# A streaming encoder step on one core: the square of a tile joins the sum one tile later, the remainder of a weight quarter is emitted with the next cast, and the planner prices a transfer by its pieces

## The chip, the cores and the metric

The kernel runs on one NeuronCore of a Trainium2 chip. The time is the device time of one launch in microseconds (us). Before the change the median of three runs is 1416.33 us (1415.28 to 1420.74). Five engines work beside each other, each through its own queue in order: TensorE (PE in the profile, with its weight loads as PEld), VectorE (DVE), ScalarE (ACT), GpSimd (POOL) and SyncE (SP), which here issues most transfers. A transfer that SP issues also waits in SP's queue for what it needs, and holds up what stands behind it.

## The reference, cut to what matters

One step of a two-layer encoder for two request groups with shared weights: 256 new frames of one stream and 32 of another, 288 columns together, at a width of 2048.

- Layer 0: adaLN (a modulation `silu(c) @ w_mod`, then RMSNorm times scale plus shift), one wide input projection, eight heads of attention with a forget gate and eight of differential attention, SiLU gates, one output projection, and `x = x + gate * out`.
- Layer 1: adaLN again, a projection to `u` and `z`, a diagonal complex state space over the positions, GELU, a GLU product, an output projection, and the residual add.
- A last RMSNorm. Every RMSNorm needs the sum of the squares of `x` over its 2048 channels:

```python
def _rmsnorm(x, g):
    x32 = x.astype(jnp.float32)
    y = x32 * lax.rsqrt(jnp.mean(x32 * x32, axis=-1, keepdims=True) + EPS)
    return (y * g.astype(jnp.float32)).astype(x.dtype)
```

All is float32, and the tolerance needs nearly that.

## The kernel before, in words

Activations lie transposed: channels on the 128 partitions, the 288 columns along the free dimension, so a width of 2048 is 16 tiles of 128x288. Full precision comes from splitting each operand into a rounded part and its remainder: a weight quarter `st[:, i, :]` (128x512) becomes `hi`, which ACT casts, and `lo = w - hi`, which DVE subtracts; an activation chunk becomes `ah` and `al` in the same way. One product of a 128x128 weight block with an activation tile is then three matmuls (`ah,hi`, `al,hi`, `ah,lo`). Here such a triple is called a step. The five projections hold 2304 steps in all, and a place in the program is given below as the number of steps that stand before it in PE's order: the input projection of layer 0 is steps 0 to 1024, its output projection 1024 to 1280, the projection to `u` and `z` 1280 to 1792, the GLU product 1792 to 2048, the last projection 2048 to 2304.

A job is 16 steps with one weight tile of 1 MB (four quarters). `pump` issues the loads of the next jobs on SP as soon as one of the four slots is free; a slot is free when the `lo` of its fourth quarter is done (`st_done`). `split_step` casts the quarters ahead of PE; eight `hi`/`lo` pairs may be alive. Between the steps `side.step` lets side tasks (Python generators) emit a piece of their work: the modulation's tail, the softmax heads, the builder of the state-space matrices (`v`, `w_ps`, `k_ps`), and in layer 1 the state space itself.

What sets the order is a planner, `Plan`. Every instruction is entered with an assumed cost as it is emitted, and each engine and the pool of DMA engines has an assumed clock. A side task is let on when the assumed time of what it waits for is past on PE's assumed clock, and when the assumed clock of DVE or ACT isn't more than 4 us ahead of PE's (`BACKLOG`). The engines then run these orders as they stand, with semaphores; the assumed times have no other effect.

The state space in layer 1 goes by groups of four tiles. `u` is written to DRAM (`ud<-MX`) and read back in two forms: regrouped in eight transfers with runs of 36 numbers (`MX<-ud`), for the products `xin_ps`; and as lagged copies (`UL<-ud`, later `W1r<-ud`, four a tile), for the products `t_ps`. DVE then runs the recurrence over `X` (`X<-X,t` and `t<-X,rot`, some hundred small instructions a group), ACT gathers `Xm`, PE makes `y_ps`, ACT copies it into `Yg`, eight transfers write that to DRAM (`yd<-Yg`), two read it back (`yx<-yd`), and GELU follows on DVE and ACT. The GLU product needs all of it, split into `ah` and `al` in four chunks; its first group of columns takes chunk 3 from step 1840 on. `xin_ps`, `t_ps` and `y_ps` stand in PE's queue between the steps of the projection, so a late transfer stops the projection too.

The output projection of layer 0 (`op_evac`) and the last projection (`fin_evac`) add each finished tile to `MX` with two DVE instructions, square the tile on ACT (`yx<-MX`), and add the square to `ssq1` on DVE. Four PSUM banks (`pm`) hold the tiles in progress: PE can't begin a fifth before DVE has emptied the first. `h1_task` then scales a chunk of `MX` into `ah` and `al` for the projection to `u` and `z`.

In the profile every instruction has line 114, since one helper (`Engine.__getattr__`) records them all; groups are told apart by their tiles.

Of the kernel before, what the change touches and what calls it, by code (L numbers as in the profile page):

```python
# [93 lines left out]
class Engine:  # L94
# [5 lines left out]
    def __getattr__(self, fn):  # L100
# [14 lines left out]
        return call  # L115

    def cost(self, fn, out, ins, outs, k):
        p = self.plan
# [3 lines left out]
        if fn == "dma_start":  # L122
            t = max([p.when(p.written, a) for a in ins] + [p.at[self.name], p.base.get(out.tensor.name, 0.0)])
            p.at[self.name] = t + (0.45 if self.name != "pool" else 1.0)
            size = n * out.shape[0] * 4 / 360e3
            if self.name == "act":
                end = t + 2.6 + 2 * size
            else:
                p.at["dma"] = max(p.at["dma"], t + 0.6) + size
                end = p.at["dma"] + 2.0  # L130
            p.note(p.written, out, end)
            for a in ins:
                p.note(p.read, a, end)
            p.last = max(p.last, end)
            return
# [118 lines left out]
def build(tc, I, O):  # L254
# [8 lines left out]
    with ExitStack() as ctx:  # L263
# [23 lines left out]
        def TT(o, a, b, op, eng=dve):  # L287
            eng.tensor_tensor(o, a, b, op=op)
# [107 lines left out]
        def st_done(k):  # L396
            del st_of[k]
            if taken and taken[0] is None:
                taken[0] = slot_of[k]
            else:  # L400
                st_free.append(slot_of[k])
# [4 lines left out]
        def split_step(t, force=False):  # L406
# [12 lines left out]
            act.copy(hi, st[:, i, :])  # L419
            TT(lo, st[:, i, :], hi.bitcast(F32), ALU.subtract)  # L420
            qs.append((hi, lo))
            split["live"] += 1
            if i == 3:
                st_done(k)
                pump()
            return True

        def order_of(j):
# [21 lines left out]
        def run_jobs(upto, n_side):  # L450
            while pos["run"] < upto:
# [5 lines left out]
                if j["kind"] == "main":  # L457
# [6 lines left out]
                    for i, (n, q, k, begin, end) in enumerate(order_of(j)):  # L464
                        while len(qs) <= q:
                            if not qs:
                                side.upto(plan.when(plan.written, st_of[t]))
                            split_step(t, True)
                        if first and begin:
                            g["ps"][n] = pm.tile([128, 512], F32, tag="m", name="m")  # L470
# [7 lines left out]
                        if last and end:  # L478
                            plan.last = 0.0
                            g["evac"](n, ps[:, 0:N], c)  # L480
                        if i % 2:
                            split_step(t)
                            side.step(n_side)
# [106 lines left out]
        def slot(k):  # L590
            return k if k < 12 else k + 4
# [753 lines left out]
        def op_evac(gi):  # L1345
            def ev(n, ps, c):
# [9 lines left out]
                if c == 3:  # L1356
                    sq = scratch(k % 2)[:, 0:T]
                    act.activation(sq, MX[:, slot(k), :], AF.Square)
                    if k == 0:
                        dve.tensor_copy(ssq1, sq)  # L1360
                    elif k < KT - 1:
                        TT(ssq1, ssq1, sq, ALU.add)
                    else:
                        ssl.append(sq)
                    if n == 3:
                        ready.add(("x1", gi))
            return ev

        ssl = []
        op0 = len(jobs)  # L1370
# [408 lines left out]
        def fin_evac(gi):  # L1779
            def ev(n, ps, c):  # L1780
# [3 lines left out]
                for b, (j0, j1) in enumerate(((0, JP), (JP, NJ))):  # L1784
                    dve.scalar_tensor_tensor(xk[:, :, j0:j1], ps.rearrange("p (s j) -> p s j", s=LC)[:, :, j0:j1],
                                             gate[:, 1, k, b:b + 1], xk[:, :, j0:j1], op0=ALU.mult, op1=ALU.add)
                sq = scratch(k % 2)[:, 0:T]
                act.activation(sq, MX[:, k, :], AF.Square)
                if k == 0:
                    dve.tensor_copy(ssq1, sq)  # L1790
                elif k < KT - 1:
                    TT(ssq1, ssq1, sq, ALU.add)
                else:
                    ssl.append(sq)
            return ev
# [192 lines left out]
```

## Time and profile before

| | before |
|---|---|
| median of 3 runs | 1416.33 us |
| profiled execution, its own time | 1416.64 us |
| its span, first to last instruction | 1414.8 us |
| PE busy | 1270.3 us (90%) |
| DVE busy | 928.9 us (66%) |
| ACT busy | 594.3 us (42%) |
| mean granted TensorE clock | 0.948 |
| DMA, mean over the span | 244 GB/s |

Engine rows give busy time, its share of the span and the number of instructions. A row of waits reads: the engine and tile that stood idle, what released it, total idle in us, number of waits, the longest. A row of the timeline gives start and length in us, the engine, the operation with output and inputs, the count of merged instructions, and in brackets the idle time before it with its releaser. SPq is SP's sequencer, which issues transfers. A step takes three rows of `m` on PE.

### The profile page before, as it was taken

To read this page: it belongs to the slowest core of one execution; us is meant where nothing else is said; L and a number is where in the kernel's file an instruction comes from. 1 tells how busy PE (TensorE), PEld (TensorE's weight loads), DVE (VectorE), ACT (ScalarE), POOL (GpSimd) and SP (SyncE) were. 2 spreads that over 40 slices of the span, in tenths; PEclk is the share of its full clock that TensorE was granted. 3 is DMA by queue.
4 is the path that set the end of the run, shared out by engine and by line. 5 is a ranking of instruction groups with operands and counts; after the bars stand their busy time and mean duration, and the time that the engine had idled before them with its cause. 6 is when DMAs were issued, how large, how long until landed. Compare 5 with 4: busy or idle time off the path is not lost.

```text
span 1414.8 us, 28189 instructions
## 1 busy us (share of the span) xinstructions
PE 1270.3 (90%) x11098; PEld 1112.1 (79%) x11098; DVE 928.9 (66%) x2212; ACT 594.3 (42%) x1394; POOL 32.6 (2%) x21
## 2 busy tenths in 40 slices
PE   4999899999998999998996978849979877999996
PEld 2788798887887888886896958838869847989995
DVE  4479988697786777887667618527735835455554
ACT  4434233333454454554535624413444534344341
POOL 0005000000000000000000000000000000000000
PEclk9999999999999999999998999978988978999998
DMA  9988696698889898987755877883587645877641
GB/s 316 339 304 309 211 329 249 227 336 293 313 289 312 287 317 298 337 296 271 272 178 137 287 200 174 226 205 104 181 188 201 197 150 155 293 258 266 230 148 68
DMA packets 251011, 344.91 MB, mean 244 GB/s; under 512 B 51424, under 2 KB 141552, under 8 KB 250880
## 3 DMA queue, kind: packets, MB, share of 16 engines
q1 hardware_dynamic: 238208, 313.47, 68.5%
q10 hardware_dynamic: 12672, 29.65, 5.9%
q8 instruction: 88, 1.44, 0.4%
q14 instruction: 43, 0.35, 0.1%
HBM read 307.13 MB, written 35.95 MB: 242 GB/s over the span
## 4 chain that ended last, share of the span: by engine, by line
issue 46%; PE 24%; DVE 13%; DMA 10%; ACT 4%; SPq 1%; ACTq 0%; POOL 0%; POOLq 0%; DVEq 0%
PE m L114 19%; DMA w<-in_w_in_att 5%; DVE lo L114 4%; PE mod_ps L114 3%; DVE v L114 2%; ACT hi L114 2%; DVE MX L114 2%; DMA w<-in_w_mod 2%; DVE tmpv L114 1%; DMA w<-in_w_out_att 1%; SPq L114 1%; DVE qkv L114 1%; DVE dtmp L114 1%; DMA v_d<-v 1%; DMA c_gT<-in_gT 0%
## 5 line engine op out<-in xcount | busy, mean ns | idle before, releaser
L114 PE MATMUL m<-ah,hi 128*128 128x288 f32 (+1 forms) x2304 | 717.2, 311 | 28.3 <-ACT ah L114 14.6
L114 PE MATMUL m<-ah,lo 128*128 128x288 f32 (+1 forms) x2304 | 691.8, 300 | 6.7 <-DVE lo L114 6.6
L114 PE MATMUL m<-al,hi 128*128 128x288 f32 (+1 forms) x2304 | 692.6, 301 | 0.4 <-DVE al L114 0.4
L114 DVE TENSOR_TENSOR lo<-w,hi 128x512 fp32r<-128x512 f32 x560 | 374.2, 686 | 246.3 <-ACT hi L114 236.0
L114 PEld LDWEIGHTS m<-ah,hi 128*128 128x128 f32 x2304 | 444.3, 193 | 94.9 <-issue 41.8
L114 ACT CAST hi<-w 128x512 fp32r<-128x512 f32 x560 | 326.5, 618 | 362.5 <-PE m L114 204.0
L114 PEld LDWEIGHTS m<-ah,lo 128*128 128x128 f32 x2304 | 444.9, 193 | 9.3 <-DVE lo L114 9.3
L114 PEld LDWEIGHTS m<-al,hi 128*128 128x128 f32 x2304 | 445.2, 193 | 1.6 <-DVE al L114 1.4
L114 PE MATMUL mod_ps<-w,cs 128*32 128x512 f32 x736 | 96.2, 617 | 1.9 <-DMA w<-in_w_mod 1.9
L114 DVE SCALAR_TENSOR_TENSOR qkv<-m,qkv 128x288 f32<-128x288 f32 x168 | 73.0, 452 | 26.4 <-PE m L114 26.1
L114 DVE TENSOR_TENSOR X<-X,t 128x32 f32<-128x32 f32 (+1 forms) x256 | 58.3, 228 | 8.2
L114 PE MATMUL t_ps<-UL,kb 128*32 128x288 f32 (+1 forms) x220 | 31.9, 431 | 26.1 <-DMA UL<-ud 26.1
L114 ACT ACTIVATE yx<-MX 128x288 f32<-128x288 f32 (+1 forms) x40 | 19.7, 492 | 70.0 <-DVE MX L114 70.0
L114 DVE TENSOR_TENSOR v<-pt,raw 128x512 f32<-128x512 f32 (+1 forms) x64 | 46.0, 718 | 2.5 <-DMA v_d<-v 2.2
L114 DVE SCALAR_TENSOR_TENSOR MX<-MX,c_dT,t_ps 128x288 f32<-128x288 f32 x16 | 8.2, 514 | 59.0 <-PE t_ps L114 59.0
L114 DVE TENSOR_TENSOR tmpv<-pt,raw 128x512 f32<-128x512 f32 (+1 forms) x64 | 45.9, 717 | 0.0
L114 PE MATMUL y_ps<-Xm,v 128*128 128x74 f32 x256 | 37.4, 309 | 9.1 <-ACT Xm L114 9.1
L114 PEld LDWEIGHTS y_ps<-Xm,v 128*128 128x128 f32 x256 | 35.9, 223 | 10.8 <-ACT Xm L114 10.3
L114 PEld LDWEIGHTS t_ps<-UL,kb 128*32 128x32 f32 x220 | 9.5, 124 | 43.6 <-DMA UL<-ud 35.2
L114 DVE SCALAR_TENSOR_TENSOR MX<-m,gate,MX 128x256 f32<-128x256 f32 x96 | 30.7, 362 | 18.7 <-PE m L114 18.6
L114 PEld LDWEIGHTS mod_ps<-w,cs 128*32 128x32 f32 x736 | 16.9, 110 | 29.4 <-issue 25.6
L114 DVE TENSOR_TENSOR v<-v,tmpv 128x512 f32<-128x512 f32 (+1 forms) x48 | 34.3, 714 | 1.7
(228 smaller groups left out, 921.1 us busy)
## 6 DMA issues: line engine op xcount, KB each, us to landing
w<-in_w_mod SPq DMA_DIRECT2D x128, 512.0 KB
w<-in_w_in_att SPq DMA_DIRECT2D x40, 1024.0 KB
w<-in_w_in_ssm SPq DMA_DIRECT2D x32, 1024.0 KB
w<-in_w_mod SPq DMA_DIRECT2D x28, 1024.0 KB
w<-in_w_in_att SPq DMA_DIRECT2D x48, 512.0 KB
w<-in_w_out_att SPq DMA_DIRECT2D x16, 1024.0 KB
w<-in_w_glu SPq DMA_DIRECT2D x15, 1024.0 KB
w<-in_w_out_ssm SPq DMA_DIRECT2D x13, 1024.0 KB
```

The lines of the kernel that those rows point to most:

```text
L114: return f(*a, **k)
```

## The change

It has three parts. (1) The `lo` subtraction of a quarter isn't emitted behind its `hi` cast any more, but is kept in `rests` and emitted at the next cast, or as soon as the planner's time for the cast is past on DVE's or PE's assumed clock (`rest_due`), or at the latest ahead of the first matmul that reads it. The release of the slot and the next load move with the fourth quarter's `lo`. (2) `squares` emits the add of a tile's square ahead of the next tile's square instead of behind its own; the first square goes straight into `ssq1`, so the copy is gone; the last one is handed on as before. (3) The planner's price of a transfer no longer is its bytes at 360 GB/s, but the number of its contiguous pieces, each at 12 plus 0.142 per number, over 16 engines; and it lets a transfer begin 1.2 instead of 0.6 us after its issue, or end 3.2 instead of 2.6 us after it on ACT's queue. For a 1 MB weight tile the price goes from 2.91 to 2.71 us, for one of the eight transfers with runs of 36 numbers from 0.205 to 0.547 us. The instructions that are executed stay the same, but for the two copies; their order on PE, DVE, ACT and SP is new over the whole program.

```diff
+    @staticmethod
+    def pieces(out, src):
+
+        total, run = 1, []
+        for d in out.shape:
+            total *= d
+        for a in (out, src):
+            r = 1
+            for st, n in reversed(list(a.ap)[1:]):
+                if st != r and n > 1:
+                    break
+                r *= n
+            run.append(r)
+        r = min(run)
+        return total / r * (12 + 0.142 * r) / 16e3
...
-            size = n * out.shape[0] * 4 / 360e3
+            size = self.pieces(out, ins[0])
             if self.name == "act":
-                end = t + 2.6 + 2 * size
+                end = t + 3.2 + 2 * size
             else:
-                p.at["dma"] = max(p.at["dma"], t + 0.6) + size
+                p.at["dma"] = max(p.at["dma"], t + 1.2) + size
                 end = p.at["dma"] + 2.0
...
             act.copy(hi, st[:, i, :])
-            TT(lo, st[:, i, :], hi.bitcast(F32), ALU.subtract)
             qs.append((hi, lo))
             split["live"] += 1
-            if i == 3:
-                st_done(k)
-                pump()
+            rest_step(0)
+            rests.append((k, i, st, hi, lo))
             return True
+        rests = []
+        def rest_step(left):
+            while len(rests) > left:
+                k, i, st, hi, lo = rests.pop(0)
+                TT(lo, st[:, i, :], hi.bitcast(F32), ALU.subtract)
+                if i == 3:
+                    st_done(k)
+                    pump()
+        def rest_due():
+            if rests and plan.when(plan.written, rests[0][3]) <= max(plan.at["dve"], plan.at["pe"]):
+                rest_step(len(rests) - 1)
...
+                        if rests and rests[0][:2] <= (t, q):
+                            rest_step(0)
...
                         if i % 2:
+                            rest_due()
                             split_step(t)
                             side.step(n_side)
...
-                    sq = scratch(k % 2)[:, 0:T]
-                    act.activation(sq, MX[:, slot(k), :], AF.Square)
-                    if k == 0:
-                        dve.tensor_copy(ssq1, sq)
-                    elif k < KT - 1:
-                        TT(ssq1, ssq1, sq, ALU.add)
-                    else:
-                        ssl.append(sq)
+                    squares(k, MX[:, slot(k), :])
...
+        def squares(k, x):
+            for sq in sqs:
+                TT(ssq1, ssq1, sq, ALU.add)
+            sqs.clear()
+            sq = scratch(k % 2)[:, 0:T] if k else ssq1
+            act.activation(sq, x, AF.Square)
+            if k == KT - 1:
+                ssl.append(sq)
+            elif k:
+                sqs.append(sq)
```

What this does to the orders is shown at three places.

DVE at the end of layer 0's output projection, where the finished tiles are added to `MX` and their squares (`yx`) to `ssq`. Before:

```order
L114 SCALAR_TENSOR_TENSOR MX<-m,gate,MX 128x8x32
L114 SCALAR_TENSOR_TENSOR MX<-m,gate,MX 128x8x4
L114 TENSOR_TENSOR ssq_123<-ssq_123,yx 128x288
L114 SCALAR_TENSOR_TENSOR MX<-m,gate,MX 128x8x32
L114 SCALAR_TENSOR_TENSOR MX<-m,gate,MX 128x8x4
L114 TENSOR_TENSOR ssq_123<-ssq_123,yx 128x288
L114 TENSOR_TENSOR lo<-w,hi 128x512
```

Now:

```order
L114 TENSOR_TENSOR lo<-w,hi 128x512
L114 SCALAR_TENSOR_TENSOR MX<-m,gate,MX 128x8x32
L114 SCALAR_TENSOR_TENSOR MX<-m,gate,MX 128x8x4
L114 TENSOR_TENSOR lo<-w,hi 128x512
L114 SCALAR_TENSOR_TENSOR MX<-m,gate,MX 128x8x32
L114 SCALAR_TENSOR_TENSOR MX<-m,gate,MX 128x8x4
L114 TENSOR_TENSOR ssq_123<-ssq_123,yx 128x288
L114 SCALAR_TENSOR_TENSOR MX<-m,gate,MX 128x8x32
```

The rows look alike, but the first add now stands behind the third tile of the sum, and reads the square of the second: the square that an add reads was begun a tile earlier. Two chunk rows (`al<-MX,scl,ah`) of `h1_task` have also moved: of the first chunk's four tiles one stood ahead of step 1280 before, and all four do now.

SP around the second write of `u` to DRAM. Before:

```order
L114 DMA ud<-MX 128x4x288
L114 DMA UL<-ud 128x1x288 x3
L114 DMA w<-in_w_in_ssm 128x4x512 x2
L114 DMA MX<-ud 16x32x36 x8
L114 DMA UL<-ud 128x1x288
```

Now:

```order
L114 DMA ud<-MX 128x4x288
L114 DMA UL<-ud 128x1x288
L114 DMA w<-in_w_in_ssm 128x4x512
L114 DMA kb<-kb_d 128x256
L114 DMA MX<-ud 16x32x36 x8
```

One weight load less stands between the write and the eight transfers that read it back. At the third write it is none instead of one.

PE around step 1792, the end of the projection to `u` and `z`. Before, behind the last `m` of 290 columns:

```order
L114 MATMUL y_ps<-Xm,v_12894 128x74 x8
L114 MATMUL t_ps<-UL,kb 32x288 x4
L114 MATMUL t_ps<-UL,kb 32x144 x4
L114 MATMUL t_ps<-UL,kb 32x288
L114 MATMUL t_ps<-W1r,kb 32x288 x3
L114 MATMUL t_ps<-UL,kb 32x144
L114 MATMUL t_ps<-W1r,kb 32x144 x3
L114 MATMUL y_ps<-Xm,v_13544 128x74 x8
L114 MATMUL t_ps<-UL,kb 32x288 x4
L114 MATMUL t_ps<-UL,kb 32x144 x4
```

Now the last `t_ps` stands 16 steps ahead of that place, between steps of the projection:

```order
L114 MATMUL y_ps<-Xm,v_12670 128x74 x8
L114 MATMUL t_ps<-UL,kb 32x288
L114 MATMUL t_ps<-W1r,kb 32x288 x3
L114 MATMUL t_ps<-UL,kb 32x144
L114 MATMUL t_ps<-W1r,kb 32x144 x3
L114 MATMUL m<-ah,hi 128x290
L114 MATMUL m<-al,hi 128x290
L114 MATMUL m<-ah,lo 128x290
```

Four `t_ps` tiles and two `y_ps` tiles stood at step 1792 with no step of a projection among them. Now the `t_ps` of tiles 10 to 15 stand at steps 1702, 1718, 1722, 1740, 1770 and 1776 (before: 1774, 1780 and four at 1792), and the `y_ps` of tiles 12 to 15 at 1776, 1780, 1788 and 1798 (before: 1776, 1784 and two at 1792). The four groups of `xin_ps` begin at steps 1394, 1466, 1504 and 1676 (before: 1388, 1472, 1512 and 1674), and the last product of the attention stands at step 1070 (before: 1152).

More of the change, by code (lines that the diff above doesn't have):

```diff
@@ L1367, in op_evac @@
             return ev
-        ssl = []
+        ssl, sqs = [], []
+        def squares(k, x):
[8 more added lines that the diff above has]
+                sqs.append(sq)
         op0 = len(jobs)
@@ L1786, in ev @@
                                              gate[:, 1, k, b:b + 1], xk[:, :, j0:j1], op0=ALU.mult, op1=ALU.add)
[L1787 to L1794, printed above, removed]
+                squares(k, MX[:, k, :])
             return ev
```

## The prediction

> **What bounds the kernel now.** I read the page first for the total, and then a table of seven stretches cut at the places where the program changes its work. Columns: start and end, length, then busy time and count on PE, PEld, DVE, ACT and POOL, the granted TensorE clock, the DMA share and GB/s.
>
> ```profile
> span 1414.8 us, 28189 instructions
> ...
> 0.00:246.00 246.00, 217.41 (x1812) 183.02 (x1813) 182.32 (x470) 93.55 (x186) 22.10 (x7) 0.97 0.84 293
> 246.00:710.00 464.00, 446.02 (x4446) 378.01 (x4448) 354.66 (x729) 220.21 (x567) 8.00 (x11) 0.99 0.86 295
> 710.00:776.00 66.00, 55.02 (x416) 52.72 (x413) 45.16 (x110) 27.59 (x61) 0.75 (x2) 0.95 0.52 159
> 776.00:1079.00 303.00, 250.24 (x2122) 229.04 (x2121) 158.06 (x494) 118.39 (x314) 0.85 (x1) 0.87 0.71 198
> 1079.00:1133.00 54.00, 49.27 (x382) 47.09 (x382) 44.20 (x146) 27.38 (x69) 0.00 (x0) 1.00 0.66 190
> 1133.00:1190.50 57.50, 41.15 (x241) 29.40 (x241) 26.80 (x44) 22.83 (x48) 0.00 (x0) 0.78 0.59 170
> 1190.50:1415.00 224.50, 211.15 (x1698) 192.80 (x1698) 117.72 (x225) 84.37 (x153) 0.85 (x1) 0.96 0.58 202
> ```
>
> The attention stretch (246 to 710) is PE's: 18.0 us of 464 are idle at a clock of 0.99. Nothing that only frees another engine can bring more than those 18 there. The losses lie elsewhere: 52.8 us idle in the first part of the state space (776 to 1079, clock 0.87), and above all 1133 to 1190.5, where PE is idle for 16.4 us of 57.5 and at 0.78 of its clock for the rest. So the sum goes by four places: the end of the output projection, the attention, the first state-space part, and the gap around step 1792.
>
> **The end of layer 0's output projection.** Groups of DVE from 733 to 772 (count, busy, mean, idle before and its releaser), then PE's waits from 735 to 776, then three rows of DVE's timeline.
>
> ```profile
> L114 DVE TENSOR_TENSOR ssq<-ssq,yx 128x288 f32<-128x288 f32 x14 | 6.4, 458 | 7.9 <-ACT yx L114 7.9
> L114 DVE COPY ssq<-yx 128x288 f32<-128x288 f32 x1 | 0.3, 309 | 0.6 <-ACT yx L114 0.6
> ```
>
> ```profile
> PE m L114 <- ACT ah L114: 7.2, 1, 7.2
> PE m L114 <- DVE MX L114: 3.8, 6, 1.1
> ```
>
> ```profile
> 770.75 0.64 DVE L114 SCALAR_TENSOR_TENSOR MX<-m,gate,MX 128x256 f32<-128x256 f32 x2
> ...
> 773.08 1.76 DVE L114 SCALAR_TENSOR_TENSOR al<-MX,scl,ah 128x256 fp32r<-128x256 f32 x6
> ```
>
> Each add waits about 0.57 us for the square begun just before it, 7.9 + 0.6 = 8.5 us in all, and DVE empties PE's four banks, so PE pays. One tile later the square has a tile's two `MX` instructions (0.64) as its cover. With the copy (0.3) DVE saves 8.8 us. Ahead of step 1280 now stand some eight more chunk rows; six last 1.76 us, so I put 2.4 us for them. The last `MX` ends at 771.4 - 8.8 + 2.4 = 765.0 in place of 771.4, and the first chunk is then complete, where before it was finished behind that (the wait of 7.2). PE resumes about 8 us earlier. Upper bound: both waits gone, 7.2 + 3.8 = 11. Lower bound: `ah` on ACT comes no earlier than the added rows allow and the last steps run in the shadow of DVE's `lo` rows, 5. **I take 8.** If the cover failed (DVE reaching the add before ACT ended), the 0.57 would be back for that tile only.
>
> **The attention.** Here the deferred `lo` matters.
>
> ```profile
> L114 DVE TENSOR_TENSOR lo<-w,hi 128x512 fp32r<-128x512 f32 x188 | 123.9, 685 | 67.9 <-ACT hi L114 67.4
> ```
>
> DVE stood 67.4 us behind `hi` with its other work queued behind it; emitted with the next cast, `lo` finds `hi` done. But PE idles only 18 us there, so the ceiling is 18, and half of it, 9, is what I would call the best. Against it: the side work now ends at step 1070 where it ended at 1152, about 13% denser, and DVE was busy 354.66 of 464 us, 76%, so 86% in the denser part: waits of PE for `lo` or `v` may appear. The `lo` rows themselves move by at most one cast, but the fourth frees the slot, so a load starts later by one cast; with four slots that is covered by the three other tiles, 16 steps each. Value 2, from -8 (half as much idle again) to +9.
>
> **The state space up to 1079.** PE's waits from 776 to 1079, the longest one, and SP around the second write of `u`:
>
> ```profile
> PE t_ps L114 <- DMA UL<-ud: 22.1, 9, 10.1
> PE xin_ps L114 <- DMA MX<-ud: 17.8, 3, 6.8
> PE y_ps L114 <- ACT Xm L114: 6.4, 3, 4.1
> PE m L114 <- DVE lo L114: 3.8, 3, 2.5
> PE xin_ps L114 <- DMA UL<-ud: 2.7, 1, 2.7
> ```
>
> ```profile
> 949.98 1.17 PE L114 MATMUL t_ps<-UL,kb 128*32 128x288 f32 x2 [10.15 <-DMA UL<-ud]
> ```
>
> ```profile
> 859.84 0.39 SPq L114 DMA_DIRECT2D ud<-MX  x1
> ...
> 866.65 6.96 SPq L114 DMA_DIRECT2D w<-in_w_in_ssm  x2
> 873.70 6.94 SPq L114 DMA_DIRECT2D MX<-ud  x8
> ```
>
> The names add to 52.8. `u` is written at 859.84 and its eight read-backs are issued only at 873.70, behind two weight loads which wait for slots. Now one load stands there instead of two, and at the third write none instead of one. Two issues of 0.4 us took 6.96 there, so the second load held the queue for about 6, and so I let two of the three waits of `xin_ps` lose their bulk: 17.8 x 2/3 = 12. Six steps of the first group's cover (1388 to 1394) are 2.4 us more. Against this the third group comes eight steps earlier (1512 to 1504, 3.2 us less cover), and the `t_ps` waits (22.1) don't have to shrink: the lagged copies stand in the same queue, behind the eight, and so three of them lose the place ahead of the weights. 12 + 2.4 - 3.2 - 2 for those = 9. Low end: the saved waits reappear at `t_ps` and every wait not named grows by a tenth, -4. High end: all of 17.8 and 2.7, 20. **I take 9.**
>
> **The gap at step 1792.** PE, then SP, then DVE:
>
> ```profile
> 1121.46 0.78 PE L114 MATMUL y_ps<-Xm,v 128*128 128x74 f32 x5 [2.31 <-ACT Xm L114]
> ...
> 1133.13 2.01 PE L114 MATMUL y_ps<-Xm,v 128*128 128x74 f32 x16 [0.35 <-ACT Xm L114]
> ...
> 1152.59 2.53 PE L114 MATMUL t_ps<-UL,kb 128*32 128x288 f32 x16
> ...
> 1162.38 0.61 PE L114 MATMUL m<-ah,hi 128*128 128x288 f32 x1
> ...
> 1163.27 0.44 PE L114 MATMUL m<-ah,hi 128*128 128x288 f32 x1
> 1163.51 0.44 PE L114 MATMUL m<-al,hi 128*128 128x288 f32 x1
> ...
> 1169.87 0.29 PE L114 MATMUL m<-ah,lo 128*128 128x288 f32 x1
> 1170.01 0.29 PE L114 MATMUL m<-ah,hi 128*128 128x288 f32 x1
> ...
> 1190.42 0.61 PE L114 MATMUL m<-ah,hi 128*128 128x288 f32 x1 [7.48 <-ACT ah L114]
> ```
>
> ```profile
> 1152.62 1.38 SPq L114 DMA_DIRECT2D X<-in_w_mod  x1
> ...
> 1162.02 0.39 SPq L114 DMA_DIRECT2D w<-in_w_glu  x1
> ...
> 1165.68 7.91 SPq L114 DMA_DIRECT2D yd<-Yg  x8
> 1177.65 0.89 SPq L114 DMA_DIRECT2D yx<-yd  x2
> ```
>
> ```profile
> 1182.16 0.76 DVE L114 TENSOR_TENSOR MX<-MX,yx 128x576 f32<-128x576 f32 x1 [1.16 <-DMA yx<-yd]
> ```
>
> From the `y_ps` at 1133.13 no step of `m` starts before 1162.38: four `t_ps` tiles and two `y_ps` tiles stand there in one block, at half clock (rows of `m` right behind it start 0.24 us apart, and 0.14 once the clock is back). The last `y_ps` is done when the `t_ps` of 1152.59 begin, and its `Yg` could be written from about 1155 on, but SP holds a `w_glu` load until 1162.02, when the last `t_ps` frees what it writes into, and the eight `yd` go out at 1165.68 only. From there to PE's resumption is 1190.42 - 1165.68 = 24.7 us: the writes, the read-back, GELU on DVE and ACT, the split.
>
> After the change no `t_ps` is left at the block, so no load waits for one. Counted from step 1792: six steps to the last `y_ps` at 1798, 6 x 3 x 0.14 = 2.5 us, that tile's 2.0 as in the row of 1133.13, 0.5 for SP to reach the first `yd`, and the 24.7: 29.7 us in place of 57.3 (1133.1 to 1190.4). Gross gain 27.6. The moved `t_ps` and `y_ps` still take PE's time, at full clock about 8 us in all (the 1152.59 row is 2.53 a tile at half clock): 20 left. What is added is their waits at the new places, among steps. The waits of `t_ps` from 1079 to 1192 were:
>
> ```profile
> PE t_ps L114 <- DMA W1r<-ud: 4.7, 6, 1.3
> PE t_ps L114 <- DMA UL<-ud: 4.0, 5, 1.5
> ```
>
> With the 22.1 from before 1079 these are 30.8 us over 16 tiles, 1.9 a tile. Six tiles at 1.3 to 1.9 are 8 to 11; I take 8, since part of it overlaps with waits that stood there already. A `t_ps` that waits also keeps DVE's recurrence waiting for its output, and DVE was 44.2 of 54 us busy just ahead. **I take 12.** High: the waits vanish and PE works at full clock under the drain, 25. Low: 0, the waits eat it all.
>
> [...]
>
> **The rest** (start, modulation, GLU product, last projection) keeps its instructions, and the last projection has steps of PE enough over its adds: 0, within 3.
>
> **Sum.** 8 + 2 + 9 + 12 + 0 = 31, against the profiled execution's own 1416.64 (its span and 1.8 us around it): 1385.6. That execution lies 0.3 us above the median of the runs, so I say 1386. All low ends at once: 5 - 8 - 4 + 0 - 3 = -10, so 1427. All high: 11 + 9 + 20 + 25 + 3 = 68, so 1349. Half of either spread is about what independent terms give: 1372 to 1402 is the forecast's own range.
>
> **The rivals.** A measurement of this kernel tells about 0.5%, 7 us, from no change.
>
> *More: the waits at `xin_ps` and `t_ps` mostly go* (chance 0.11). The third and fourth terms near their tops, 20 + 20 with 8 and 8: 56, so 1360. For it: idle and half clock together are the largest loss in the trace. Against: the 10.15 us wait at `t_ps` is on a transfer whose place hardly moves.
>
> *The transfers are late anyway* (0.16). The reordering on SP moves the issue, not the landing; `UL` and `MX` come when the DMA engines are through, and the waits reappear at other names. For it: the eight `yd` take 7.91 us to issue and 4 more until their read-back can start. Only the squares count: 1416.6 - 8 = 1408.6, just beyond the 0.5%.
>
> *Slower: six `t_ps` in the stream block PE and DVE* (0.14). Each waits in PE's queue ahead of steps and of the `y_ps` of its group. The squares' 8 and the gap's 20 are used up when the six waits come to 28 us, 4.7 each; beyond that it is a loss. At 6.4 each, 38 us: 1416.6 + 10 = 1427. For it: the 10.15 row shows such a wait, and the copies of the last tiles have less time. Against: 11 waits from 1079 on had none above 1.5.
>
> *The attention takes it back* (0.09). Denser side work makes DVE the pace there: the 8 us of its low end plus the state space at 0 and the waits of the gap at 2: 8 - 8 + 2, so 1414, no change. Against: 76% busy.
>
> That the adds don't move is excluded by the order.
>
> **Numbers.** Forecast 0.50, more 0.11, late anyway 0.16, slower 0.14, attention 0.09. Faster: 0.50 + 0.11 + 0.09 of "late anyway" = 0.70. Same: 0.07 + 0.08 = 0.15. Slower: 0.14 + 0.01 = 0.15. The range of 8 in 10 goes from 1360 to 1416: below it about half of "more", above it most of "slower".
>
> **What would show it.** Squares: no idle of DVE behind `yx` in the output projection, and the first `m` behind step 1280 about 8 us nearer to the last `MX`. Attention: PE idle within 10 to 26 us, DVE's 67 behind `hi` much less. State space: the read-back issued within some 7 us of the second write, and the `xin_ps` waits near 6. Gap: from step 1792 to the first product with chunk 3 (step 1840), before 57.3 us and the 48 steps that fit into it, now under 45, with a clock above 0.78, and short waits at six `t_ps`. The prediction is wrong if the `t_ps` waits from step 1700 on exceed 28 us, or if PE's idle in the attention grows beyond 26.

## The result, and the profile after

The changed kernel takes 1382.93 us (median of 4 runs, 1380.97 to 1384.47), beside 1415.8 us of the kernel before on the same chip (4 runs, 1413.05 to 1420.74). The ratio is 0.9763, with a 95% interval of 0.9733 to 0.9793: faster. The forecast was 1386, its own range 1372 to 1402.

From the page of the kernel after, the span, and then the table of stretches, cut at the same places of the program as below (columns as in the table of before):

```profile
span 1378.9 us, 28204 instructions
```

```profile
0.00:240.67 240.67, 214.00 (x1779) 177.71 (x1779) 178.49 (x463) 92.21 (x184) 22.11 (x7) 0.97 0.87 301
240.67:702.69 462.02, 448.33 (x4457) 380.92 (x4453) 357.00 (x736) 221.64 (x568) 8.78 (x12) 0.99 0.86 296
702.69:802.68 99.99, 97.79 (x795) 96.17 (x792) 69.18 (x169) 54.32 (x128) 0.85 (x1) 1.00 0.72 231
802.68:1029.26 226.58, 184.61 (x1564) 164.54 (x1563) 125.73 (x424) 84.94 (x230) 0.00 (x0) 0.87 0.69 188
1029.26:1125.10 95.84, 80.69 (x660) 66.88 (x659) 59.04 (x171) 39.04 (x96) 0.00 (x0) 0.88 0.68 202
1125.10:1154.96 29.86, 21.13 (x162) 20.90 (x160) 16.09 (x27) 17.37 (x39) 0.00 (x0) 0.89 0.72 170
1154.96:1378.90 223.94, 210.67 (x1698) 192.39 (x1698) 116.70 (x225) 84.54 (x153) 0.85 (x1) 0.96 0.59 205
```

The cuts are the first product of steps 400, 1152, 1388, 1674, 1792 and 1840. The same steps in the kernel before begin at 241.52, 708.08, 825.62, 1060.04, 1133.13 (there the block of `t_ps` and `y_ps`, the step itself only at 1162.38) and 1190.42. The difference of the spans, 35.9 us, is made up so:

| steps | before, us | after, us | gain, us |
|---|---|---|---|
| 0 to 400 | 241.5 | 240.7 | 0.9 |
| 400 to 1152, attention | 466.6 | 462.0 | 4.5 |
| 1152 to 1388, end of layer 0 | 117.5 | 100.0 | 17.6 |
| 1388 to 1674, state space | 234.4 | 226.6 | 7.8 |
| 1674 to 1792 | 73.1 | 95.8 | -22.8 |
| 1792 to 1840, the block | 57.3 | 29.9 | 27.4 |
| 1840 to the end | 224.4 | 223.9 | 0.4 |

PE's waits in the kernel after (total, times, longest), from step 1152 to 1388, from 1388 to 1674, and from 1674 to just past 1840:

```profile
PE m L114 <- DVE lo L114: 1.4, 2, 0.7
PE rstd_ps L114 <- DVE yx L114: 0.5, 1, 0.5
PE m L114 <- DVE MX L114: 0.3, 1, 0.3
```

```profile
PE t_ps L114 <- DMA UL<-ud: 30.0, 10, 6.6
PE m L114 <- ACT hi L114: 6.5, 1, 6.5
PE m L114 <- DVE lo L114: 3.5, 1, 3.5
```

```profile
PE t_ps L114 <- DMA UL<-ud: 13.7, 9, 3.0
PE m L114 <- ACT ah L114: 8.7, 1, 8.7
PE t_ps L114 <- DMA W1r<-ud: 1.4, 1, 1.4
```

At the end of layer 0 the waits of 7.2 and 3.8 are down to 2.2 in all. In the state space the waits of `xin_ps` are gone, and those of `t_ps` have grown from 22.1 to 30.0 there. From step 1674 on `t_ps` waits in the stream for 15.1 us: 10.7 of them at the six tiles that were moved (steps 1702 to 1776), and 4.4 at tile 9, which stands at step 1680 (1682 before) and did not wait there before. 8.7 us are still waited at step 1840, where the drain of the last group ends.

### The profile page after: what moved, and what is told of

It is laid out like the page before. It is cut to its first block, busy times and chain, and to the rows that moved or that the text cites. A ratio compares the mean times of both kernels' runs of the same rounds, so it can differ in the third digit from the quotient of the medians.

```text
span 1378.9 us, 28204 instructions
## 1 busy us (share of the span) xinstructions
PE 1257.2 (91%) x11098; PEld 1099.5 (80%) x11098; DVE 922.2 (67%) x2210; ACT 594.1 (43%) x1394; POOL 32.6 (2%) x21
## 4 chain that ended last, share of the span: by engine, by line
issue 45%; PE 35%; DMA 9%; DVE 8%; ACT 2%; SPq 1%; ACTq 0%; POOL 0%; POOLq 0%; DVEq 0%
PE m L114 27%; PE mod_ps L114 4%; DMA w<-in_w_in_att 3%; DMA v_d<-v 2%; DVE lo L114 2%; DMA w_d<-W 1%; DVE v L114 1%; DVE MX L114 1%; DVE qkv L114 1%; PE w_ps L114 1%; ACT hi L114 1%; SPq L114 1%; DVE dtmp L114 1%; DMA w<-in_w_mod 1%; DVE tmpv L114 1%
## 5 line engine op out<-in xcount | busy, mean ns | idle before, releaser
L114 ACT CAST hi<-w 128x512 fp32r<-128x512 f32 x552 | 322.3, 618 | 357.2 <-PE m L114 221.0
L114 DVE TENSOR_TENSOR lo<-w,hi 128x512 fp32r<-128x512 f32 x552 | 367.2, 685 | 158.2 <-ACT hi L114 156.1
L114 PE MATMUL mod_ps<-w,cs 128*32 128x512 f32 x744 | 99.2, 626 | 15.3 <-DVE ssq L114 13.2
L114 DVE SCALAR_TENSOR_TENSOR qkv<-m,qkv 128x288 f32<-128x288 f32 x168 | 73.3, 450 | 28.1 <-PE m L114 27.8
L114 PE MATMUL t_ps<-UL,kb 128*32 128x288 f32 (+1 forms) x220 | 38.4, 454 | 43.7 <-DMA UL<-ud 43.7
L114 DVE TENSOR_TENSOR v<-pt,raw 128x512 f32<-128x512 f32 (+1 forms) x64 | 45.9, 718 | 19.8 <-DMA v_d<-v 15.6
L114 DVE TENSOR_TENSOR tmpv<-pt,raw 128x512 f32<-128x512 f32 (+1 forms) x64 | 45.8, 716 | 0.0
L114 DVE TENSOR_TENSOR t<-X,rot 128x64 f32<-128x64 f32 x144 | 33.2, 240 | 1.7
L114 PE MATMUL y_ps<-Xm,v 128*128 128x74 f32 x256 | 30.7, 273 | 1.1 <-ACT Xm L114 1.1
```

The lines of the kernel that those rows point to most:

```text
L114: return f(*a, **k)
```

## The experiments

Each ran beside the kernel before on the same chip; the ratio is to that, with its 95% interval, from 4 to 10 runs.

| run | median, us | before, us | ratio (interval) |
|---|---|---|---|
| squares alone | 1412.13 | 1413.37 | 0.9995 (0.9970 to 1.0019) |
| all but squares | 1392.69 | 1413.37 | 0.9842 (0.9804 to 0.9880) |
| deferral of `lo` alone | 1388.72 | 1413.37 | 0.9817 (0.9778 to 0.9856) |
| price alone | 1376.06 | 1413.37 | 0.9730 (0.9696 to 0.9763) |
| all but deferral | 1375.80 | 1413.57 | 0.9725 (0.9674 to 0.9775) |
| all but price | 1373.13 | 1413.57 | 0.9717 (0.9662 to 0.9772) |
| change, `t_ps` 3 us later | 1349.48 | 1413.57 | 0.9533 (0.9486 to 0.9580) |
| change, `yd` on two queues | 1374.41 | 1413.57 | 0.9730 (0.9682 to 0.9778) |
| change, `t_ps` 5 us later | 1338.53 | 1414.75 | 0.9467 (0.9429 to 0.9505) |
| change, `t_ps` 6 us later | 1376.72 | 1414.75 | 0.9735 (0.9701 to 0.9769) |
| change, all landings 2 us later | 1357.81 | 1414.75 | 0.9608 (0.9574 to 0.9642) |
| all but price, `t_ps` 4 us later | 1358.37 | 1414.75 | 0.9608 (0.9575 to 0.9642) |

### The squares, alone and taken out

The first run adds only part (2) to the kernel before. The second takes it out of the changed kernel:

```diff
-            for sq in sqs:
-                TT(ssq1, ssq1, sq, ALU.add)
-            sqs.clear()
-            sq = scratch(k % 2)[:, 0:T] if k else ssq1
+            sq = scratch(k % 2)[:, 0:T]
             act.activation(sq, x, AF.Square)
-            if k == KT - 1:
-                ssl.append(sq)
-            elif k:
-                sqs.append(sq)
+            if k == 0:
+                dve.tensor_copy(ssq1, sq)
+            elif k < KT - 1:
+                TT(ssq1, ssq1, sq, ALU.add)
+            else:
+                ssl.append(sq)
```

The places of `t_ps` and `xin_ps` stay those of before in the first, and those of the change in the second.

> The kernel before with the squares' part alone: lo stays behind its cast, and transfers are priced by bytes. In the order the four t_ps and two y_ps still stand in one block at step 1792. Theory (the places add up): only the end of the output projection gains, 8 us of waits and some 4 more because PE keeps its clock behind step 1281, so 1416 - 12 = 1404 (1400 to 1408), with PE's waits for MX and ah there near 1 us, and the 57 us gap at step 1792 still there. Rival (the whole gain comes from the new plan, the squares only move the wait): within 3 us of before.

> The changed kernel with the squares' part undone; the places of t_ps, y_ps and xin_ps in PE's order are those of the changed kernel. Theory (the places add up): the 12 us come back and nothing else, 1383 + 12 = 1395 (1391 to 1399); the t_ps waits and the 30 us from step 1792 to 1840 stay. Rival: the earlier start of the state space pays again later, within 3 us of the change.

Alone, the squares bring nothing that can be measured, as the rival of the first expectation had it; taken out of the change, they cost 9.8 us. Why, is read on DVE. Groups of DVE from 725 to 775 us (busy, mean, idle before and its releaser), first of the kernel before:

```profile
L114 DVE TENSOR_TENSOR lo<-w,hi 128x512 fp32r<-128x512 f32 x22 | 14.9, 690 | 4.8 <-ACT hi L114 4.2
...
L114 DVE TENSOR_TENSOR ssq<-ssq,yx 128x288 f32<-128x288 f32 x14 | 6.4, 458 | 7.9 <-ACT yx L114 7.9
```

then with the squares alone:

```profile
L114 DVE TENSOR_TENSOR lo<-w,hi 128x512 fp32r<-128x512 f32 x22 | 14.9, 690 | 10.9 <-ACT hi L114 10.9
...
L114 DVE TENSOR_TENSOR ssq<-ssq,yx 128x288 f32<-128x288 f32 x14 | 6.3, 450 | 0.0
```

with all but the squares:

```profile
L114 DVE TENSOR_TENSOR lo<-w,hi 128x512 fp32r<-128x512 f32 x21 | 13.7, 685 | 0.9 <-ACT hi L114 0.9
...
L114 DVE TENSOR_TENSOR ssq<-ssq,yx 128x288 f32<-128x288 f32 x14 | 6.4, 459 | 7.9 <-ACT yx L114 7.9
```

and in the changed kernel:

```profile
L114 DVE TENSOR_TENSOR ssq<-ssq,yx 128x288 f32<-128x288 f32 x14 | 6.3, 447 | 0.0
...
L114 DVE TENSOR_TENSOR lo<-w,hi 128x512 fp32r<-128x512 f32 x27 | 18.2, 683 | 0.5
```

With the squares alone, the wait only changes its name. Here is one tile of that run, first on ACT, then on DVE:

```profile
757.62 0.44 ACT L114 ACTIVATE yx<-MX 128x288 f32<-128x288 f32 x1 [0.48 <-DVE MX L114]
757.97 0.60 ACT L114 CAST hi<-w 128x512 fp32r<-128x512 f32 x1
759.94 0.44 ACT L114 ACTIVATE yx<-MX 128x288 f32<-128x288 f32 x1 [1.37 <-DVE MX L114]
```

```profile
757.44 0.45 DVE L114 TENSOR_TENSOR ssq<-ssq,yx 128x288 f32<-128x288 f32 x1
758.60 0.69 DVE L114 TENSOR_TENSOR lo<-w,hi 128x512 fp32r<-128x512 f32 x1 [0.71 <-ACT hi L114]
759.21 0.64 DVE L114 SCALAR_TENSOR_TENSOR MX<-m,gate,MX 128x256 f32<-128x256 f32 x2
```

ACT can begin the square only when DVE has added the tile to `MX`, and casts `hi` right behind it; DVE no longer waits for the square, and stands at `lo` for the cast that is queued behind that square. ACT then waits 1.37 us for DVE's next tile. The two engines go in lockstep, and one of DVE's two waits a tile is enough to keep them so. Only with both gone does DVE run free.

The length of the stretch from step 1152 to 1388 bears this out over all eight ways to combine the three parts. It takes 117.5 us before, 116.5 with the squares alone, 111.7 with the deferral alone and 112.6 with the price alone; 111.2 with deferral and price, 111.7 with squares and price; and 100.1 and 100.0 in the two kernels that have both squares and deferral. (The first two still have the first group of `xin_ps` in this stretch, some 4 us.)

### The deferral alone and the price alone

The kernel before with part (1) alone, and with part (3) alone.

> The kernel before with the deferral of lo alone. Its order also dissolves the block: the last t_ps stands at step 1696, the last y_ps at 1732, and the attention ends at step 1072. Theory (the block is what costs, whatever dissolves it): the gap's 27 us come in, some 20 to 25 go out again as t_ps waits in the stream, the attention gives 4: 1416 - 8 = 1408 (1395 to 1415). Rival (the price of the pieces is what makes the state space better): no gain or a loss, since t_ps and xin_ps come earlier than their transfers, 1416 to 1435.

> The kernel before with the price by pieces and the later start of a transfer alone. The last t_ps stands at step 1754, the last y_ps at 1744, the attention ends at step 1162. Theory (the block is what costs): as with the deferral alone, the gap's 27 us in and some 20 out, the first part of the state space 8 better: 1416 - 14 = 1402 (1392 to 1412). Rival (the deferral carries it): within 7 us of before.

Both gain more than was expected, 25 and 37 us, and both medians lie below the ranges given. Either part dissolves the block at step 1792. The expectations named the places of the last `y_ps`, 1732 and 1744 (1798 in the change), but not what they are worth: the drain behind it is then covered, nearly or wholly, by steps, and step 1792 to 1840 takes 19.3 us with the deferral alone and 20.5 with the price alone, against 29.9 in the change. The difference between the two is made ahead of step 1674, which begins 31.6 us later than before with the deferral alone and 4.5 earlier with the price alone. From there to step 1792 the deferral alone is the shorter one, 57.0 against 70.4 us; it has 15 of the 16 `t_ps` ahead of step 1674, and the price alone 11.

### Pairs

All but the deferral, which emits `lo` behind its cast again:

```diff
-            rest_step(0)
             rests.append((k, i, st, hi, lo))
+            rest_step(0)
```

All but the price:

```diff
-            size = self.pieces(out, ins[0])
+            size = n * out.shape[0] * 4 / 360e3
             if self.name == "act":
-                end = t + 3.2 + 2 * size
+                end = t + 2.6 + 2 * size
             else:
-                p.at["dma"] = max(p.at["dma"], t + 1.2) + size
+                p.at["dma"] = max(p.at["dma"], t + 0.6) + size
```

> The changed kernel with lo emitted behind its cast again. Theory, formed from the two runs on the squares (1412 alone, 1393 without them): at the end of the output projection DVE waits for ACT twice a tile, for the square and for the next hi, and taking one wait away only lengthens the other (13.3 us of both before, 10.9 with the squares alone, 9.4 with the deferral alone, 0.5 with both). Then the squares bring nothing without the deferral: 1376 like the price alone (1372 to 1380), with DVE's waits for hi near 10 us there. Rival (the squares are worth their 10 us with any plan that isn't the one of before): 1366 (1362 to 1370).

> The changed kernel with transfers priced by bytes and begun 0.6 us after the issue again, so squares and deferral together; the places of t_ps and y_ps are those of the deferral alone. Theory (squares and deferral belong together): the deferral alone gave 1388.7, and both bring the 10 us that the changed kernel has over the one without the squares: 1379 (1375 to 1383). Rival (the squares need the new price too): 1389 (1385 to 1393).

DVE from 725 to 775 us in the run without the deferral:

```profile
L114 DVE TENSOR_TENSOR lo<-w,hi 128x512 fp32r<-128x512 f32 x24 | 16.2, 690 | 12.1 <-ACT hi L114 12.1
...
L114 DVE TENSOR_TENSOR ssq<-ssq,yx 128x288 f32<-128x288 f32 x14 | 6.3, 450 | 0.0
```

So the squares add nothing to the price (1375.8 against 1376.1), as the lockstep says, and 15.6 us to the deferral (1373.1 against 1388.7), where 10 had been expected. Between the profiles of these two, steps 1152 to 1388 differ by 11.6 us, and the time ahead of step 1152 by 5.8, which one profile of each doesn't settle. The parts don't add up in the other way either: the deferral on top of the price makes it slower by 16.6 us (1392.7 against 1376.1, intervals of the ratios apart). In the profiles step 1388 to 1674 becomes 12.1 us shorter by it, but step 1674 to 1792 25.2 longer, with two more `t_ps` tiles behind 1674, and step 1792 to 1840 9.4 longer, with the last `y_ps` at 1798 in place of 1744: the loss lies where the places have moved. With all three, the kernel is no faster than with the price alone, or with the first two alone; the intervals of the change and of these two touch or overlap, so which of the three is best isn't settled.

### What the moved `t_ps` cost, and how far they may be moved

In the change, PE's loss from step 1674 to 1792 took back most of the block's gain. The planner decides by an assumed landing when a `t_ps` may be emitted; this makes it think 3 us later of the copies of a tile, and touches nothing else:

```diff
-                plan.last = max([...] + [plan.when(plan.written, kb)])
+                plan.last = max([...] + [plan.when(plan.written, kb)]) + 3.0
                 yield "dve"
```

> The changed kernel, with the planner told that the lagged copies of a tile land 3 us later than it assumes; nothing else. In the order the sixteen t_ps are spread from step 1402 to 1736, the last y_ps stands at 1702 and not at 1798. Theory (t_ps stands too early for its copies, and the last y_ps too late for the drain to be covered): PE's waits at t_ps fall from 45 us to under 25, the wait of 8.7 us at step 1840 goes, and PE keeps more of its clock: 1383 - 20 - 8 = 1355 (1345 to 1367). Rival (the copies are late because the buffers that they land in come free late, so that a later t_ps makes the next copies later): the waits stay over 35 us, and the time between 1370 and 1390.

1349.48 us: 33 us less than the change. PE's waits from step 1388 to 1840, with 3 us:

```profile
PE t_ps L114 <- DMA UL<-ud: 13.2, 9, 4.8
PE t_ps L114 <- DMA W1r<-ud: 12.3, 7, 4.1
PE xin_ps L114 <- DMA UL<-ud: 8.8, 2, 5.9
PE xin_ps L114 <- DMA MX<-ud: 5.3, 1, 5.3
```

The waits of `t_ps` are 25.5 us in place of 45.1, and there is none at step 1840: 19.6 + 8.7 = 28.3 us less. But waits at `xin_ps`, 14.1 us, came back on the way, so this isn't 28 of the 33: from step 1388 to 1840 PE's idle time fell by 20.1 us in all (65.9 to 45.8), and its busy time by 7.3, with a granted clock of 0.90 from 802 to 1050 us and of 0.96 from 1050 to 1130 us of that execution, in place of 0.87, 0.88 and 0.89 in the change's three stretches from step 1388 to 1840.

With 5 us and with 6 us:

> As the run with the lagged copies 3 us later, now 5 us. The sixteen t_ps are spread from step 1402 to 1772, the last y_ps stands at 1716. Theory (waits at t_ps and the place of the last y_ps set it): waits at t_ps fall further, from 25 us to under 18, and the drain stays covered: 1349 - 5 = 1344 (1338 to 1350). Rival (each us of delay past 3 delays the buffers instead): 1352 to 1365.

> The same with 6 us, one more. The order tips over: four t_ps stand at step 1792 in one block again and two more at 1774 and 1780, though the last y_ps stands at 1768. Theory (a block at step 1792 costs whatever makes it, since PE has nothing else there and its copies are late): the stretch from step 1760 to 1840, 32 us in the run with 3 us, is over 45 us again, and the time 1360 to 1375. Rival (only the y_ps behind the block made it costly before): the stretch stays under 37 us, and the time below 1352.

With 5 us PE's waits at `t_ps` are these, and the kernel takes 1338.53 us, within the range given and the best of all:

```profile
PE t_ps L114 <- DMA UL<-ud: 7.9, 6, 3.3
...
PE t_ps L114 <- DMA W1r<-ud: 2.2, 3, 1.5
```

With 6 us it takes 1376.72, just beyond the range given. Until step 1760 that kernel is ahead of the one with 5 us (1073.5 against 1078.7 us into the execution); then the block is back, with four `t_ps` at step 1792. PE's busy time, clock, DMA share and GB/s of that run from step 1760 to the block, in the block, and from there to step 1840:

```profile
1073.52:1100.09 26.57, 23.73 (x162) 0.87 0.70 176
1100.09:1135.92 35.83, 19.89 (x65) 0.56 0.51 146
1135.92:1156.37 20.45, 20.45 (x146) 0.94 0.62 208
```

35.8 us for 64 small products and one of `m`, at 0.56 of the clock, and 82.85 from step 1760 to 1840, where over 45 had been expected. The last `y_ps` stood at 1768 there, ahead of the block, and no time was lost at step 1840. So the block costs by itself: nothing of the projection stands in it, the `t_ps` in it wait for copies 13 times, 15.6 us in all, and the clock over it was 0.56.

### The drain behind the last `y_ps`

Every second one of the last eight writes goes to ACT's queue:

```diff
-                        sp.dma_start(dst[s], Yg[16 * s:16 * s + 16])
+                        (act if s % 2 and i == KT - 1 else sp).dma_start(dst[s], Yg[16 * s:16 * s + 16])
```

> The changed kernel, with every second one of the last eight writes of Yg issued on ACT's queue instead of SP's; the orders on PE and DVE stay. Theory (from the last y_ps to step 1840 one chain sets the time, 24 us, of which 6.9 are the issues on SP): half of these 6.9 go, PE's wait of 8.7 us at step 1840 falls to about 5, and the time by 3 to 4, 1379. Rival (the read-back waits for the DMA engines, not for the issue): the wait stays above 8, and the time within 2 us of the change.

PE at step 1840, in the changed kernel and then with two queues:

```profile
1154.96 0.61 PE L114 MATMUL m<-ah,hi 128*128 128x288 f32 x1 [8.73 <-ACT ah L114]
```

```profile
1147.28 0.61 PE L114 MATMUL m<-ah,hi 128*128 128x288 f32 x1 [5.00 <-ACT ah L114]
```

The wait falls by 3.73 us, the size that was expected, but only in part by the way that was expected. Here is SP's queue, again first in the changed kernel and then with two queues (there ACT issues the other four writes, from 1126.64 to 1129.70):

```profile
1131.18 6.94 SPq L114 DMA_DIRECT2D yd<-Yg  x8
...
1143.80 1.31 SPq L114 DMA_DIRECT2D yx<-yd  x2
```

```profile
1127.29 5.41 SPq L114 DMA_DIRECT2D yd<-Yg  x4
...
1138.54 0.89 SPq L114 DMA_DIRECT2D yx<-yd  x2
```

From the end of the last `y_ps` to the issue of the read-back it is 13.1 us with two queues and 14.4 in the change, so at most 1.3 us come from the writes: the four that are left on SP took 5.41 us, and not half of 6.94. The other 2.4 us lie behind the issue of the read-back, 8.7 us from there to step 1840 in place of 11.2, and what shortened that isn't shown. The run's median is 8.5 us under the change's, measured beside another run of before, and its ratio's interval overlaps the change's; in its profile 4 us of that were there at step 1152 already, so the row carries the verdict, and the total doesn't.

From the end of the last `y_ps` to step 1840 the chain takes 25.6 us in the change (1129.39 to 1154.96). At 0.40 us a step (three rows of `m`, 0.13 us apart behind step 1840 once the clock is back at 1.00) some 64 steps would cover it, so the last `y_ps` would have to stand at 1776 or before. Most places agree: 1798 with 8.7 us of wait; with the `t_ps` 6, 5 and 3 us later, at 1768, 1716 and 1702, and with the deferral alone, at 1732, there is none. But at 1744, with the price alone and with all but the deferral, 2.9 us were waited although 96 steps follow. With the price alone the chain took 40.8 us: the read-back was issued at 1123.23, 17.5 us behind the `y_ps`, and DVE and ACT did other work, on the tiles `SZ` and `zt`, between it and the last split at 1147.78. So the number of steps is not all; what stands in between in the queues of SP, DVE and ACT can stretch the chain.

### Two ways that gave less

```diff
-                end = p.at["dma"] + 2.0
+                end = p.at["dma"] + 4.0
```

is the later landing for all transfers of SP and POOL; the other run is all but the price with the lagged copies 4 us later.

> The changed kernel with every transfer of SP and POOL assumed to land 2 us later, not only the lagged copies. xin_ps starts at step 1414 in place of 1394, t_ps is spread from 1416 to 1772, the last y_ps stands at 1762. Theory (the assumed landing is too early for all the small transfers): the waits at xin_ps nearly go as well, and those at t_ps are under 25 us: 1345 (1336 to 1355). Rival (all later means only that the chain starts later): the waits move behind step 1760, 1360 to 1385.

> Squares and deferral with the price by bytes, as in the run without the price part (1373), and the lagged copies 4 us later. t_ps is spread from step 1398 to 1782, the last y_ps stands at 1748. Theory (the price part matters only through the places that it gives): as good as with the price by pieces, 1373 - 25 = 1348 (1340 to 1358). Rival (the price by pieces is needed, the xin_ps waits of 14 to 18 us for MX stay without it): 1360 to 1372.

Both came to 1358, 10 to 13 us above what the theory gave and just outside its range, and a little below that of the rival. With all landings later the `xin_ps` waits nearly went (2.8 us are left), but those of `t_ps` were 30.1, and step 1152 began at 713.1 us, in place of 698.2 to 705.0 in the change and in four kernels with its order up to there; the attention has transfers too, and that their new prices cost this is argued, not shown. Without the price by pieces the waits at `t_ps` fell to 16.6 us, from 37.3, but those at `xin_ps` stayed, 26.0 without the 4 us and 28.1 with them:

```profile
PE xin_ps L114 <- DMA MX<-ud: 28.1, 4, 8.8
```

That part of the rival holds: the price by pieces does matter for the eight transfers with runs of 36 numbers. The change, with the same squares and deferral, has none of these waits.

## Why the prediction was right, and where its terms were not

The sum was 31 us, and 35.9 are measured between the profiled executions. The total was right in part by luck: the first term brought 9.6 us more than forecast and the last 7.3 less. The stated range is also narrower than its own rule: half of either spread gives 1367 to 1406, and not 1372 to 1402; 1382.93 lies in both. The four terms, in their order:

**The end of the output projection, forecast 8.** The waits of 7.2 + 3.8 fell to 2.2: 8.8 us, as sized. The stretch gained 17.6, above the upper bound of 11, since 2.7 us were the first wait of `xin_ps`, 1.1 its products (moved behind step 1388), and 5 PE's busy time, nearly all of it the low clock behind the long wait (0.50 from 773.11 to 782.64), which the sum had left out. But the step "One tile later the square has a tile's two `MX` instructions (0.64) as its cover. With the copy (0.3) DVE saves 8.8 us" named the wrong cause: by itself this saves nothing, because DVE meets ACT again at `lo`. It took the deferral, which the prediction had counted in the attention alone. So the waits that go were sized right, and the mechanism that was to take them away was not right. For the same reason the price under "Only the squares count" was wrong: alone they are worth 0, not 8.

**The attention, forecast 2.** 4.5 in these two executions. PE's idle time went from 18.0 to 13.7 us, within the range given; DVE's wait for `hi` halved, to 34.5, and PE gained little from it. Steps up to 1152 keep their order in four more runs, which reach step 1152 at 698.2 to 705.0 us; before it was 708.1, and 706.8 with the squares alone. The gain is 3 to 10, and its size isn't settled better. Nor is it shown to be the deferral's: with the price but without the deferral step 1152 begins at 703.9 and 708.7.

**The state space, forecast 9.** 7.8, and 10.5 with the first wait of `xin_ps`. It isn't made up as said: all of the `xin_ps` waits went, not two thirds, the waits at `t_ps` grew by 7.9 and not by 2, PE had a new wait of 6.5 for `hi`, and its waits for `Xm` ahead of `y_ps` fell from 6.4 to 1.1, which the sum had not counted. The read-back was issued 8.8 us behind the second write, in place of 13.9. SP's queue in the kernel after:

```profile
834.93 0.71 SPq L114 DMA_DIRECT2D ud<-MX  x1
...
843.70 6.69 SPq L114 DMA_DIRECT2D MX<-ud  x8
```

**The gap at step 1792, forecast 12.** From step 1792 to 1840 29.9 us are measured, and 29.7 were forecast, by the same pieces: the eight writes were issued at 1131.18, 23.8 us before step 1840 (24.7 before). What was added from step 1674 to 1792 is 22.8 us, against 8 + 8 = 16, and so 4.7 us are left of 12. "What is added is their waits at the new places" was sized nearly right: the six tiles waited for 10.7 us, within the 8 to 11 that were worked out, of which the sum took the 8. With the 4.4 at tile 9, which the sum didn't have, and without the waits of before, PE's idle time rose by 10.3 us (4.9 to 15.2). The term that was mis-sized most is the work, "at full clock about 8 us in all": PE's busy time there rose by 12.5 us (68.2 to 80.7), at a clock of 0.88 and not at full clock; 1.1 of them are a group of `xin_ps` that stood ahead of step 1674 before. (The block of before was at half clock only for a part of its 29 us: its mean was 0.69.) The rival with the waits of `t_ps` as a loss needed 28 us of them at the six tiles; 10.7 came. No wait there was above 3.0 us.

Across the waits of the first three of these tiles PE ran at half clock for a part of the time, so from 1059.61 to 1069.85. The stretch around them (busy time, clock, DMA share, GB/s):

```profile
1056.00:1088.00 32.00, 21.26 (x119) 0.77 0.63 183
```

Several waits of 1 to 3 us came close together there, and the clock was 0.77. At the end of layer 0 PE ran at half clock for 9.5 us of nearly unbroken work behind the 7.2 us wait of before (the last section has the rows), and in the kernel after, where no wait was above 0.7 us, the clock was 1.00 over the stretch. There the clock worked for the change and not against it.

So two errors cancel: at the end of layer 0 the sum left out 5 us of clock and 3.8 of `xin_ps`, and from step 1674 to 1792 4.5 us of work and 2.3 of idle time. And the split by parts, which the runs made and the prediction didn't, shows that none of the three parts has a gain of its own to be added: 1412, 1389 and 1376 alone, 1383 together.

## What to carry to other kernels

Where two engines hand each other work twice a tile, taking one of the two waits away can move the time into the other, as it did here (7.9 us at `yx` gone, 4.2 at `hi` grown to 10.9); look at who stands behind whom at the next meeting before a wait is counted as a gain. Where a planner sets the order, look first at the places that it gives to the work that waits for transfers: here a single assumed time of 5 us took 1383 to 1339 us, more than the whole change had brought, and 6 us gave most of it back. A chain at the end of a stage needs enough steps behind its last piece, here some 64: count them, and look at what else stands in the queues that the chain goes through.

## What the runs showed of the hardware

In the kernel before, PE ran at half clock for 9.5 us behind the 7.2 us wait at the end of layer 0. Its matmuls at the wait and behind it:

```profile
773.11 0.61 PE L114 MATMUL m<-ah,hi 128*128 128x290 f32 x1 [7.17 <-ACT ah L114]
...
774.42 0.45 PE L114 MATMUL m<-ah,hi 128*128 128x290 f32 x1
774.66 0.45 PE L114 MATMUL m<-al,hi 128*128 128x290 f32 x1
...
782.69 0.29 PE L114 MATMUL m<-ah,lo 128*128 128x290 f32 x1
782.82 0.29 PE L114 MATMUL m<-ah,hi 128*128 128x290 f32 x1
```

The matmuls of `m` start 0.24 us apart for 9.5 us and 0.13 us after that, without a wait of note in between (some 1.3 us of these are small products for the RMSNorm): some 4 us lost on top of the 7.2, as an estimate from these two distances. Behind the 8.7 us wait of the changed kernel half clock lasted 3.6 us, from 1154.96 to 1158.60. Behind its wait of 3.5 us, which ended at 959.38, PE first ran at full clock for 1.2 us, and only then came 3.4 us at half clock (columns as in the tables of stretches):

```profile
959.38:960.62 1.24, 1.24 (x9) 1.24 (x10) 1.17 (x5) 0.00 (x0) 0.00 (x0) 1.00 0.00 0
960.62:964.03 3.41, 3.41 (x16) 3.41 (x15) 3.29 (x9) 0.78 (x2) 0.00 (x0) 0.50 0.36 62
```

So the rows right behind this wait show nothing of the low clock that follows; whether it came from the wait isn't shown. In the clock records of the two traces, before and after, every stretch at half clock, leaving out the end of the execution, is 3.41, 6.83, 10.24, 13.65, 17.07 or 20.48 us long: the one around the 7.2 us wait lasts 13.65 us, from 768.99 within the wait to 782.64, and the one around the 8.7 us wait 10.24, from 1148.36 to 1158.60. What sets how long such a stretch lasts isn't settled.
